# Three feed-forward layers as one hand-ordered list, eight column pairs by seven products for eight

## The chip, the cores and the metric

The kernel runs on one core of a Trainium2 chip. The number that counts is the device time of one execution in microseconds, as the median of several runs. Rows of the trace come from one profiled execution. In them PE is the matmul engine, PEld its loading of weights, DVE the vector engine, ACT the scalar engine, POOL the general engine; SP issues the transfers from memory.

## The reference

A diffusion backbone of two layers works on 256 noisy tokens with a prefix of 256 context tokens, width 1024. Each layer is a half-weighted SwiGLU feed-forward block (FFN), a mixer of three branches, and a second FFN; every sub-layer has a shift, a scale and a gate from a conditioning vector (nine modulations a layer). The last FFN needs the 256 noisy tokens only.

```python
def modulate(h, shift, scale):
    return h * (1.0 + scale) + shift

def swiglu(h, w1, w3, w2):
    return (jax.nn.silu(h @ w1) * (h @ w3)) @ w2
...
D_MODEL = 1024
SEQ = 256
DEPTH = 2
CTX_LEN = 256
D_FF = 2816
N_MOD = 9
```

## The kernel before

All is fp32. A factor x is split into x_hi, rounded, and x_lo = x - x_hi, and each product of 128 rows is three matmuls, hi·hi, lo·hi and hi·lo (`mm3`, L280 to L282). A block of weights of 512 KB (`wraw`) is loaded by SP, cast to `whi` by ACT (L285) and subtracted to `wlo` by DVE (L286). The tokens stand across: a matmul has 512 columns where an FFN works on all tokens, 256 where on half.

The hidden width 2816 is 11 column pairs of 256 columns of w1 and of w3. `ffn` takes six of them and then their part of the down product into the residual (`to_residual`), then the other five and theirs; the sum goes into `xT` with the gate `gmod` (L510), one group of 256 output columns at a time, four groups. The gated product `gt` (L616) is itself split into `ghi` and `glo`.

The modulations of later sub-layers are worked out in the background. `ada` loads 512 KB a step (`wada`), and a step is two DVE operations of 128x1024 (L208 the first, L210 the others); eight steps make a modulation, which the small product `pa` (L214), a copy `mrow` and four transposes (L219) then close. `tick` in `ffn` sets how many steps follow each unit of work; 16 modulations are done so, 6, 5 and 5 in the FFNs (0,0), (0,1) and (1,0).

The last output group of an FFN is the handover: products of half width, so that the norm of the first half of the tokens (`ms_f`, L319, then ACT and DVE to `hhi` and `hlo`) runs while PE does the second half, and then the first products of the next stage begin. In the handover the order on PE, DVE and ACT is that of the code; elsewhere a scheduler orders. The lines that set the work around `ms_f` are these:

```python
product(1, 0, 0, 5)
st.close(0)
product(1, 0, 5)
...
if i == 0:
    product(1, 1)
```

`product(t, d, a, b)` does the chunks a to b-1 of output half d for token half t, three matmuls a chunk; there are ten chunks in the last pass of `ffn`. `st.close(0)` issues `ms_f`.

Of the kernel before, what the change touches and what calls it, by code (L numbers as in the profile page):

```python
# [79 lines left out]
def dit_kernel(ctx: ExitStack, tc: tile.TileContext, I: dict, out: bass.AP):  # L80
# [4 lines left out]
    xp = ctx.enter_context(tc.tile_pool(name="xp", bufs=1))  # L85
    hp = ctx.enter_context(tc.tile_pool(name="hp", bufs=1))
    wr = ctx.enter_context(tc.tile_pool(name="wr", bufs=4))
    wh = ctx.enter_context(tc.tile_pool(name="wh", bufs=4))
    sm = ctx.enter_context(tc.tile_pool(name="sm", bufs=2))
    ps = ctx.enter_context(tc.tile_pool(name="ps", bufs=2, space=bass.MemoryType.PSUM))  # L90

    ctx.enter_context(tc.tile_pool(name="shift", bufs=1)).tile([P, 8], F32, name="shift")
# [15 lines left out]
    xr = [xi.tile([P, D], F32, name=f"xr{t}") for t in range(4)]  # L108
# [62 lines left out]
    def ada_first(q, c32):  # L171
# [3 lines left out]
        for k in range(0, KD, 2):  # L175
            ws.append(xi.tile([P, 2, 2, L], F32, tag="wada", name="wada", bufs=16))
            for m in range(2):
                sy.dma_start(ws[-1][:, :, m], rowsof(I["w_ada"][0], k, 2, m * D + q * L, L))
# [10 lines left out]
        mrow = xi.tile([P, P], F32, tag="mrow", name="mrow")  # L189
# [10 lines left out]
    def ada(l, m, pool):  # L200

        acc = pool.tile([P, 2, D], F32, tag="aacc", name="aacc")
        for k in range(KD):
            w = wr.tile([P, D], F32, tag="wr", name="wada")
            sy.dma_start(w, I["w_ada"][l, k * P:(k + 1) * P, m * D:(m + 1) * D])
            for t in range(2):
                if k == 0:
                    v.tensor_scalar_mul(acc[:, t], w, cs[:, k, t:t + 1])  # L208
                else:
                    v.scalar_tensor_tensor(acc[:, t], w, cs[:, k, t:t + 1], acc[:, t], op0=ALU.mult, op1=ALU.add)  # L210
            yield
        pa = psum_bg(f"pa{l}_{m}")
        for q in range(4):
            te.matmul(pa[32 * q:32 * q + 32, 0, :], ones32, acc[:, q % 2, (q // 2) * 512:(q // 2 + 1) * 512],  # L214
                      start=True, stop=True, tile_position=(0, 32 * q))
        mrow = pool.tile([P, 512], F32, tag="mrow", name="mrow")
        v.tensor_copy(mrow, pa[:, 0, :])
        for b in range(4):
            te.transpose(pa[:, 1, b * P:(b + 1) * P], mrow[:, b * P:(b + 1) * P], ident)  # L219
        v.tensor_tensor(modT[l][:, m].rearrange("p (h b) t -> p h b t", h=2),  # L220
# [4 lines left out]
        yield  # L225
# [34 lines left out]
    def split(srcs, nk, n, own=None, eng=v):  # L260

        pool, tag = own or (wh, "w")
        raw = load_raw(srcs, nk, n) if isinstance(srcs, list) else srcs
        if tag == "v":
            hi, lo = (pool.tile([P, 3, NTOK], F32R, tag=f"v{i}", name=x).rearrange("p a b -> p (a b)")[:, 0:nk * n]
                      .rearrange("p (k n) -> p k n", k=nk) for i, x in enumerate(("whi", "wlo")))
        else:
            hi = pool.tile([P, nk, n], F32R, tag=tag + "hi", name="whi")
            lo = pool.tile([P, nk, n], F32R, tag=tag + "lo", name="wlo")
# [55 lines left out]
    class Norm:  # L325

        def __init__(self, name, l, n, nt):
            self.name, self.l, self.n, self.nt = name, l, n, nt
            self.raw = {}

            self.shift = 48 if name in ("m1", "f11") else 0

        def places(self):
            self.hi, self.lo = (hp.tile([P, KD * NTOK + 256], F32R, tag=x, name=f"{x}_{self.name}")
# [191 lines left out]
    def load(w, kt, c0, r0=0, pool=None, tags=()):  # L526

        return [(split([rowsof(w, r0 + k, min(4, kt - k), c0, 2 * P)], min(4, kt - k), 2 * P,
                       pool and (pool, tags[k // 4])), k, min(4, kt - k))
                for k in range(0, kt, 4)]  # L530

    def to_residual(w, kt, x, nt, gate, st, pool, tags, r0=0, entry=None):

        for cg in range(4):
            if st is not None and cg == 3:
                chunks = load(w, kt, cg * 2 * P, r0, pool, tags)
# [38 lines left out]
    def ffn(l, f, nt, norm, mods, then):  # L575


# [3 lines left out]
        with tc.tile_pool(name=f"ffn{l}{f}", bufs=1) as fp:  # L581
            if nt == NTOK:
                fp.tile([P, 208], F32, name="pad0")
            for x in ("ghi", "glo"):
                fp.tile([P, 12, NTOK], F32R, tag=x, name=x)
            fp.tile([P, 208], F32, name="pad1")
            steps = (ada(*m, fp) for m in mods)
            pending[:] = [x for x in steps]
            total = len(mods) * (KD + 1)
            state = [0, 0]  # L590

            def tick():
                state[0] += 1
                want = min(total, -(-total * state[0] // 56))
                with norm.done():
                    background(want - state[1])
                state[1] = max(want, state[1])

            for half, (g0, g1) in enumerate(((0, 6), (6, 11))):
                nk = 2 * (g1 - g0)  # L600
                ghi = fp.tile([P, 12, NTOK], F32R, tag="ghi", name="ghi")
                glo = fp.tile([P, 12, NTOK], F32R, tag="glo", name="glo")
                for g in range(g0, g1):
                    p1, p3 = norm.accs if g == 0 else (psum("p1"), psum_bg("p3"))
                    if g > 0:
                        for acc, w in ((p1, w1), (p3, w3)):
                            product(acc, load(w, KD, g * 2 * P), (hhi, hlo), nt)
                            tick()
                            tick()
                    j = slice(2 * (g - g0), 2 * (g - g0) + 2)  # L610
                    gt = fp.tile([P, 2, NTOK], F32, tag="gt", name="gt")[:, :, 0:nt]
                    if g == 0 and norm.early:
                        norm.gated(gt)
                    else:
                        s.activation(gt, p1[:, :, 0:nt], AF.Silu)
                        v.tensor_tensor(gt, gt, p3[:, :, 0:nt], ALU.mult)  # L616
                    split_act(ghi[:, j, 0:nt], glo[:, j, 0:nt], gt)
                for _ in to_residual(w2, nk, (ghi, glo), nt, gmod[l][:, f], st if half else None, fp, ("a", "b", "c"), 2 * g0,
                                     then):
                    tick()  # L620
# [73 lines left out]
    def mixer(l, nq, entry, then):  # L694
# [35 lines left out]
        with tc.tile_pool(name=f"mx{l}", bufs=1) as mp:  # L730
            if shared:
                mp.tile([P, 208], F32, name="pad")
            br = [mp.tile([P, n, nq], F32, name=f"br{i}_{l}") for i, n in enumerate((2, 3, 3))]
# [39 lines left out]
            dk = [mq.tile([P, NTOK], F32, name=f"dk{j}") for j in range(3)]  # L773
# [53 lines left out]
            rv = mq.tile([P, 4, HEADS * DV], F32, tag="v0", name="rv")  # L827
# [9 lines left out]
            dv = mq.tile([P, 4, HEADS * DV], F32, name="dv")  # L837
# [3 lines left out]
            dq = [mq.tile([P, nq], F32, name=f"dq{j}") for j in range(3)]  # L841
# [190 lines left out]
            def merged(n, get, pool):  # L1032
                w, nk = wb[n]
                bh = pool.tile([P, 3, NTOK], F32R, tag="v0", name="bh")[:, 0:nk, 0:nq]
                bl = pool.tile([P, 3, NTOK], F32R, tag="v1", name="bl")[:, 0:nk, 0:nq]
# [170 lines left out]
```

## Time and profile before

| | us |
|---|---|
| median of 3 runs | 1994.27 (1992.68 to 1994.87) |
| profiled execution | 2003.08 |
| its span in the trace | 2001.3 |

The profiled execution is 0.44% longer than the median; the trace's span leaves out 1.8 us around it. PE is busy 1970.8 us of the span, DVE 1331.5, ACT 836.5. The mean granted clock of PE is 0.994 of full speed.

### The profile page before, as it was taken

The page shows a single profiled execution, that of the slowest core. Times are in us where ns is not written, and L with a number is a line of the kernel's source. Part 1 is how long each engine was busy: PE and PEld are TensorE (multiplying, and loading weights), DVE is VectorE, ACT ScalarE, POOL GpSimd, SP SyncE. Part 2 cuts the span into 40 slices and gives each one's busy share as a digit, 9 for nine tenths or more (in the row PEclk, how much of TensorE's full clock was granted, in tenths as well). Part 3 has the DMA queues.
Part 4 walks back from the last instruction along what each step waited for, and adds up shares of the span by engine and source line. Part 5 has one row for each costly group of instructions (what it writes and reads, how often), then busy time and mean ns, then how long its engine had stood idle before and what let it go on. Part 6 is the DMA issues. An engine that isn't in the chain of part 4 may idle for free.

```text
span 2001.3 us, 27970 instructions
## 1 busy us (share of the span) xinstructions
PE 1970.8 (98%) x11087; PEld 1684.3 (84%) x11087; DVE 1331.5 (67%) x2038; ACT 836.5 (42%) x1286; POOL 52.2 (3%) x32
## 2 busy tenths in 40 slices
PE   7999999999999999999999999999999998999998
PEld 5888888898777788988888898888888988899998
DVE  5876666576588655765666566664665779877555
ACT  3432222365476444422122343222223758666443
POOL 2000000000001110000000000000000001210000
PEclk8999999999999999999999999999999999999999
DMA  9755555422213324354555426554553234465663
GB/s 289 220 178 178 179 166 181 116 96 84 77 53 94 123 89 120 118 163 148 179 169 158 137 74 187 177 154 136 158 169 105 75 95 129 144 203 161 187 185 113
DMA packets 240507, 288.47 MB, mean 144 GB/s; under 512 B 14368, under 2 KB 222328, under 8 KB 240120
## 3 DMA queue, kind: packets, MB, share of 16 engines
q1 hardware_dynamic: 240376, 286.69, 46.7%
q8 instruction: 87, 1.43, 0.3%
q14 instruction: 44, 0.36, 0.1%
HBM read 283.50 MB, written 3.15 MB: 143 GB/s over the span
## 4 chain that ended last, share of the span: by engine, by line
PE 91%; DVE 4%; ACT 2%; DMA 2%; issue 1%; POOL 0%; SPq 0%; DVEq 0%; ACTq 0%; POOLq 0%
PE p L280 14%; PE p L282 14%; PE p L281 14%; PE py L280 8%; PE py L282 8%; PE py L281 8%; PE pg L282 3%; PE pg L281 3%; PE pg L280 3%; PE pj L281 2%; PE pj L280 2%; PE pj L282 2%; PE pv L819 1%; PE pv L821 1%; PE pv L820 1%
## 5 line engine op out<-in xcount | busy, mean ns | idle before, releaser
L285 ACT CAST whi<-wraw 128x1024 fp32r<-128x1024 f32 (+2 forms) x408 | 406.9, 1002 | 931.9 <-PE p L281 399.0
L286 DVE TENSOR_TENSOR wlo<-wraw,whi 128x1024 fp32r<-128x1024 f32 (+2 forms) x380 | 444.9, 1176 | 341.0 <-ACT whi L285 339.9
L280 PE MATMUL p<-hhi_f,whi 128*128 128x512 f32 (+1 forms) x1440 | 515.6, 358 | 0.4 <-DVE hhi_f L355 0.4
L282 PE MATMUL p<-hhi_f,wlo 128*128 128x512 f32 (+1 forms) x1440 | 512.9, 356 | 1.2 <-DVE wlo L286 0.7
L281 PE MATMUL p<-hlo_f,whi 128*128 128x512 f32 (+1 forms) x1440 | 513.5, 357 | 0.2
L280 PEld LDWEIGHTS p<-hhi_f,whi 128*128 128x128 f32 x1440 | 271.1, 188 | 48.3 <-ACT whi L285 5.9
L282 PEld LDWEIGHTS p<-hhi_f,wlo 128*128 128x128 f32 x1440 | 271.1, 188 | 41.0 <-POOL wlo L286 1.3
L281 PEld LDWEIGHTS p<-hlo_f,whi 128*128 128x128 f32 x1440 | 272.4, 189 | 39.0 <-DVE hlo_f L360 1.0
L210 DVE SCALAR_TENSOR_TENSOR aacc<-wada,cs,aacc 128x1024 f32<-128x1024 f32 x224 | 277.2, 1279 | 42.0 <-DMA wada<-w_ada 41.8
L280 PE MATMUL py<-ghi,whi 128*128 128x512 f32 (+1 forms) x764 | 266.9, 349 | 0.0
L281 PE MATMUL py<-glo,whi 128*128 128x512 f32 (+1 forms) x764 | 265.5, 347 | 0.0
L282 PE MATMUL py<-ghi,wlo 128*128 128x512 f32 (+1 forms) x764 | 265.3, 347 | 0.0
L280 PEld LDWEIGHTS py<-ghi,whi 128*128 128x128 f32 x764 | 143.4, 188 | 23.0 <-issue 4.2
L281 PEld LDWEIGHTS py<-glo,whi 128*128 128x128 f32 x764 | 144.5, 189 | 18.1
L282 PEld LDWEIGHTS py<-ghi,wlo 128*128 128x128 f32 x764 | 143.6, 188 | 18.3
L280 PE MATMUL pg<-hhi_m,whi 128*128 128x512 f32 (+1 forms) x384 | 132.4, 345 | 0.0
L282 PE MATMUL pg<-hhi_m,wlo 128*128 128x512 f32 (+1 forms) x384 | 130.3, 339 | 1.4 <-DVE wlo L286 1.4
L281 PE MATMUL pg<-hlo_m,whi 128*128 128x512 f32 (+1 forms) x384 | 130.1, 339 | 0.0
L286 POOL TENSOR_TENSOR wlo<-wraw,whi 128x768 fp32r<-128x768 f32 (+2 forms) x28 | 52.0, 1862 | 1722.2 <-ACT whi L285 1669.0
L510 DVE SCALAR_TENSOR_TENSOR xT<-py,gmod,xT 128x256 f32<-128x256 f32 x136 | 59.0, 477 | 51.8 <-PE py L282 51.4
L281 PE MATMUL pj<-hlo_m,whi 128*128 128x256 f32 (+1 forms) x288 | 92.3, 320 | 0.3 <-DVE hlo_m L360 0.2
L280 PE MATMUL pj<-hhi_m,whi 128*128 128x256 f32 (+1 forms) x288 | 92.4, 321 | 0.0
(270 smaller groups left out, 2528.6 us busy)
## 6 DMA issues: line engine op xcount, KB each, us to landing
wraw<-ffn_w SPq DMA_DIRECT2D x256, 512.0 KB, 3.9
wada<-w_ada SPq DMA_DIRECT2D x128, 512.0 KB, 3.7
wraw<-w_in SPq DMA_DIRECT2D x64, 512.0 KB, 3.6
wada<-w_ada SPq DMA_DIRECT2D x32, 256.0 KB, 6.9
wraw<-w_out SPq DMA_DIRECT2D x16, 512.0 KB, 3.5
wraw<-w_in SPq DMA_DIRECT2D x16, 384.0 KB, 3.4
wraw<-w_in SPq DMA_DIRECT2D x20, 256.0 KB, 3.0
wraw<-ffn_w SPq DMA_DIRECT2D x16, 256.0 KB, 2.7
```

Source lines behind the costliest of these rows:

```text
L210: v.scalar_tensor_tensor(acc[:, t], w, cs[:, k, t:t + 1], acc[:, t], op0=ALU.mult, op1=ALU.add)
L280: te.matmul(o, a, xh, start=start, stop=False)
L281: te.matmul(o, a, xl, start=False, stop=False)
L282: te.matmul(o, b, xh, start=False, stop=stop)
L285: s.copy(hi, src)
L286: eng.tensor_tensor(lo, src, hi.bitcast(F32), ALU.subtract)
L510: v.scalar_tensor_tensor(X[0][:, d, c], acc, gate[:, d, t:t + 1], X[0][:, d, c], op0=ALU.mult, op1=ALU.add)
L819: te.matmul(o, hhi[:, kk, ts], hi[:, k], start=(kk == 0), stop=False)
L820: te.matmul(o, hhi[:, kk, ts], lo[:, k], start=False, stop=False)
L821: te.matmul(o, hlo[:, kk, ts], hi[:, k], start=False, stop=(kk == KD - 1))
```

## The change

The three FFNs on 512 tokens become `ffn_both`; the fourth keeps the old plan. `ffn_both` builds one list of units of 24 matmuls, and `pipeline` issues it with the order on PE, DVE and ACT as written: the splits for a unit are issued three units ahead, at most three loads are outstanding, and DVE's background steps are dealt out by a `cost` of each unit.

- Column pair 0 is done in the handover as before, pairs 1 and 2 as ordinary units of 512 columns. Pairs 3 to 10 are done by `seven`: a product of 2 by 2 blocks by seven block products in place of eight, in the form with 15 additions. A block product is 24 matmuls of 256 columns.
- The sums of weight blocks are s1 and s3, made by a transfer that adds into its destination (issued by POOL after SP's plain load of the same tile), and s2 and s4, made by DVE. The forms of the tokens (`Forms`) are made once an FFN. Results of block products are copied by ACT (`keep`) and added by DVE (`add`).
- The down product is in three passes, after pairs 3, 7 and 10, of 8, 8 and 6 chunks; the last group of the third is the handover.
- A modulation is closed in pieces (`ada_end`), one per unit, in the list. In the first two FFNs the first residual needs a gate whose steps are forced in before it (`need`). The modulations are now 4, 2 (at the end of the first mixer), 5 and 5.
- Pools are laid out anew; `wr`, which holds raw loads, has 5 places for 4.

```diff
+    def seven(fm, wa, wb, c0, fp, done):
...
+        def both(tag, first, second):
+
+            t = x[tag] = fp.tile([P, 4, 2 * P], F32, tag=tag, name=tag, bufs=2)
+            sy.dma_start(t, rowsof(first[0], 4 * first[1], 4, c0, 2 * P))
+            gp.dma_start(t, rowsof(second[0], 4 * second[1], 4, c0, 2 * P), accum_op=ALU.add)
...
+        cost = 0.14
+        return [
+            Unit(part("b", fm.b11, True), whole("a11"), first_loads, 1, 0, [keep("q1", "b")], cost=cost),
+            Unit(part("c", fm.t1, True), whole("s1"), None, 0, 0, [keep("p5", "c")], cost=cost),
+            Unit(part("b", fm.t2), summed("s2", "s1", "a11"), None, 0, 1, [keep("w1", "b")], cost=cost),
+            Unit(part("a", fm.b21, True), whole("a12"), raw("a12", wa, 1), 1, 0, [add("q1", "a")], [silu(0, "q1")], cost=cost),
+            Unit(part("b", fm.t3), whole("s3"), None, 0, 0, [add("p5", "b")], cost=cost),
+            Unit(part("c", fm.b22), summed("s4", "s2", "a12"), None, 0, 1, [add("w1", "c")], [silu(1, "w1")], cost=cost),
+            Unit(part("b", fm.t4), whole("a22"), raw("a22", wb, 1), 1, 1, [gate(0, "b"), gate(1, "p5")],
+                 [lambda: done(x["gt"])], cost=cost)]
...
+            units = ordinary(1) + ordinary(2)
+            for c0, c1 in ((3, 4), (4, 8), (8, 11)):
+                g0 = 0 if c0 == 3 else c0
+                for c in range(c0, c1):
+                    units += seven(fm, w1, w3, c * 2 * P, fp, to(c - g0))
+                for cg in range(4 if c1 < KF // 2 else 3):
+                    units += down(cg, 2 * g0, 2 * (c1 - g0), c1 == KF // 2, KD if first and cg == g0 == 0 else None)
```

The loop of `pipeline`, which sets the order at each unit (`now` of the unit before, the next splits, the closing pieces, the background steps, `end` of the unit before, the unit's matmuls):

```diff
+            for i in range(len(units) + 1):
+                prev = units[i - 1] if i else None
+                if prev:
+                    if prev.need is not None:
+                        while did < prev.need and step():
+                            did += 1
+                        finish(True)
+                    for f in prev.now:
+                        f()
+                while pi < min(len(units), i + 4):
...
+                    units[pi].w = units[pi].prep()
...
+                finish()
+                if i < len(units):
+                    want += units[i].cost * scale
+                    while did < min(total, int(want + 1e-6)) and step():
+                        did += 1
+                if prev:
+                    for f in prev.end:
+                        f()
```

On DVE one column pair of the FFN (0,1) looked like this before (one gate `gt`, four splits `wlo`, the split `glo`, and adaLN products `aacc`):

```order
L286 TENSOR_TENSOR wlo<-wraw,whi 128x1024
L210 SCALAR_TENSOR_TENSOR aacc<-wada,cs,aacc 128x1024 x3
L286 TENSOR_TENSOR wlo<-wraw,whi 128x1024
L210 SCALAR_TENSOR_TENSOR aacc<-wada,cs,aacc 128x1024
L616 TENSOR_TENSOR gt<-gt,p_7318 128x1024
L286 TENSOR_TENSOR wlo<-wraw,whi 128x1024
L286 TENSOR_TENSOR glo<-gt,ghi 128x1024
```

With the change, in the same FFN, one column pair of `seven` reads so (`s_...` are tiles with added loads, `half_...` and `w_...` hold sums and kept results, L739 is a sum of weights, L761 an add, L776 a gate):

```order
L325 TENSOR_TENSOR wlo<-wraw,whi 128x1024
L240 SCALAR_TENSOR_TENSOR aacc<-wada,cs,aacc 128x1024 x2
L761 TENSOR_TENSOR half_7676<-p_8798,half_7676 128x512
L325 TENSOR_TENSOR wlo<-s_8782,whi 128x1024
L761 TENSOR_TENSOR w_7677<-p_8798,w_7677 128x512
L739 TENSOR_TENSOR half_7676<-s_8782,wraw 128x1024
L325 TENSOR_TENSOR wlo<-half_7676,whi 128x1024
L776 SCALAR_TENSOR_TENSOR gt<-p_8798,gt 128x2x256
L776 SCALAR_TENSOR_TENSOR gt<-half_7676,gt 128x2x256
L325 TENSOR_TENSOR wlo<-wraw,whi 128x1024
L325 TENSOR_TENSOR glo<-gt,ghi 128x1024
L325 TENSOR_TENSOR wlo<-s_8787,whi 128x1024
```

A sum L739 and the split of its result stand next to each other, and adds and gates from PSUM stand between the splits.

Still on DVE in the FFN (0,1), this is the place of the first pass of the down product up to its first residual, L547; it begins with the gates of column pair 3:

```order
L776 SCALAR_TENSOR_TENSOR gt<-half_7676,gt 128x2x256
L325 TENSOR_TENSOR wlo<-wraw,whi 128x1024
L240 SCALAR_TENSOR_TENSOR aacc<-wada,cs,aacc 128x1024 x2
L325 TENSOR_TENSOR glo<-gt,ghi 128x1024
L325 TENSOR_TENSOR wlo<-wraw,whi 128x1024
L240 SCALAR_TENSOR_TENSOR aacc<-wada,cs,aacc 128x1024 x6
L257 COPY mrow<-pa_8_8294 128x512
L262 TENSOR_TENSOR modT_117<-pa_8_8294,biasT_118 128x16
L190 TENSOR_SCALAR gmod_123<-modT_117 128x16
L547 SCALAR_TENSOR_TENSOR xT<-py,gmod_123,xT 128x256 x4
```

The last three steps of the modulation stand together ahead of the residual that uses its gate. Before, this modulation was closed among the column pairs, long before the first residual.

On PE the end of the same pass reads so (`py` is the down product, `p_...` the first unit of the next column pair):

```order
L319 MATMUL py<-ghi,whi 128x512
L320 MATMUL py<-glo,whi 128x512
L321 MATMUL py<-ghi,wlo 128x512
L253 MATMUL pa_0_8554<-aacc,ones_107 32x512 x4
L753 MATMUL p_8559<-hhi_f_7218,whi 128x256
L753 MATMUL p_8559<-hlo_f_7219,whi 128x256
L753 MATMUL p_8559<-hhi_f_7218,wlo 128x256
```

Before, the same product stood among matmuls of one down group:

```order
L280 MATMUL py<-ghi,whi 128x512
L281 MATMUL py<-glo,whi 128x512
L282 MATMUL py<-ghi,wlo 128x512
L214 MATMUL pa_0_7660<-aacc,ones_102 32x512 x4
L280 MATMUL py<-ghi,whi 128x512
L281 MATMUL py<-glo,whi 128x512
```

It has moved to the end of the pass. What DVE does ahead of it, from the residual of the third output group to that of the fourth, is this with the change:

```order
L547 SCALAR_TENSOR_TENSOR xT<-py,gmod_123,xT 128x256 x4
L325 TENSOR_TENSOR wlo<-s_8342,whi 128x1024
L240 SCALAR_TENSOR_TENSOR aacc<-wada,cs,aacc 128x1024 x2
L739 TENSOR_TENSOR half_7676<-s_8342,wraw 128x1024
L325 TENSOR_TENSOR wlo<-half_7676,whi 128x1024
L240 SCALAR_TENSOR_TENSOR aacc<-wada,cs,aacc 128x1024 x4
L547 SCALAR_TENSOR_TENSOR xT<-py,gmod_123,xT 128x256 x4
```

The splits here already belong to the next column pair, and the last two steps of the modulation stand behind them.

## Rows read from the trace of the kernel before

**Rows 1.** The page: busy time by engine, and the chain that ended last.

```profile
PE 1970.8 (98%) x11087; PEld 1684.3 (84%) x11087; DVE 1331.5 (67%) x2038; ACT 836.5 (42%) x1286; POOL 52.2 (3%) x32
...
PE 91%; DVE 4%; ACT 2%; DMA 2%; issue 1%; POOL 0%; SPq 0%; DVEq 0%; ACTq 0%; POOLq 0%
```

**Rows 2.** Windows by stage: FFN (0,0), mixer, FFN (0,1), FFN (1,0).

```profile
core 0: us, PE busy (x) PEld busy (x) DVE busy (x) ACT busy (x) POOL busy (x), PEclk, DMA share, GB/s
48.00:400.00 352.00, 351.48 (x1612) 286.98 (x1613) 245.72 (x319) 105.46 (x118) 0.47 (x1) 1.00 0.58 175
412.00:806.00 394.00, 390.56 (x1962) 319.43 (x1961) 263.70 (x503) 213.84 (x392) 20.84 (x12) 1.00 0.29 92
806.00:1184.00 378.00, 377.48 (x1860) 315.07 (x1860) 238.56 (x291) 115.95 (x149) 0.00 (x0) 1.00 0.48 148
1188.00:1555.00 367.00, 367.00 (x1781) 305.14 (x1781) 229.61 (x266) 109.12 (x133) 0.00 (x0) 1.00 0.50 151
```

**Rows 3.** Timeline of the handover after the FFN (0,1): start, length.

```profile
1172.55 0.64 PE L319 MATMUL ms_f<-acc_f,ones 128*128 128x256 f32 x2
...
1172.84 0.47 PE L280 MATMUL py<-ghi,whi 128*128 128x256 f32 x1
...
1173.22 0.47 ACT L290 ACTIVATE acc_f<-ms_f,eps 128x256 f32<-128x256 f32 x1 [1.25 <-PE ms_f L319]
...
1173.73 0.42 DVE L291 SCALAR_TENSOR_TENSOR rtmp<-ms_f,acc_f 128x256 f32<-128x256 f32 x1 [1.30 <-ACT acc_f L290]
...
1175.11 1.43 DVE L341 TENSOR_TENSOR h<-xT,acc_f 128x256 f32<-128x256 f32 x4
...
1177.51 0.75 DVE L360 TENSOR_TENSOR hlo_f<-h,hhi_f 128x256 fp32r<-128x256 f32 x2
...
1178.33 0.28 PE L280 MATMUL p<-hhi_f,whi 128*128 128x256 f32 x1
```

**Rows 4.** Timeline of PE, two gapless stretches: their first and last products.

```profile
299.75 0.39 PE L280 MATMUL p<-hhi_f,whi 128*128 128x512 f32 x1
...
314.48 0.39 PE L282 MATMUL p<-hhi_f,wlo 128*128 128x512 f32 x1
...
1899.69 0.28 PE L281 MATMUL py<-glo,whi 128*128 128x256 f32 x1
...
1903.93 0.28 PE L281 MATMUL py<-glo,whi 128*128 128x256 f32 x1
```

**Rows 5.** Timeline of DVE in the FFN (1,0).

```profile
1331.62 1.65 DVE L510 SCALAR_TENSOR_TENSOR xT<-py,gmod,xT 128x256 f32<-128x256 f32 x4
1333.19 2.35 DVE L286 TENSOR_TENSOR wlo<-wraw,whi 128x1024 fp32r<-128x1024 f32 x2
...
1392.68 0.68 DVE L217 COPY mrow<-pa 128x512 f32<-128x512 f32 x1
...
1394.69 6.06 DVE L210 SCALAR_TENSOR_TENSOR aacc<-wada,cs,aacc 128x1024 f32<-128x1024 f32 x5
```

**Rows 6.** Groups by line and shape: busy us, mean ns of one, idle before.

```profile
L286 DVE TENSOR_TENSOR wlo<-wraw,whi 128x1024 fp32r<-128x1024 f32 x340 | 413.7, 1221 | 293.5 <-ACT whi L285 292.5
...
L1065 DVE SCALAR_TENSOR_TENSOR gt<-gt,pb 128x512 f32<-128x512 f32 x16 | 10.3, 684 | 13.6 <-PE pb L282 13.6
...
L285 ACT CAST whi<-wraw 128x1024 fp32r<-128x1024 f32 x344 | 360.4, 1052 | 843.4 <-PE p L281 387.5 <-PE py L281 218.7 <-DMA wraw<-ffn_w 120.7
```

**Rows 7.** Timeline of PE around the close of a modulation.

```profile
1390.26 0.39 PE L282 MATMUL p<-hhi_f,wlo 128*128 128x512 f32 x1
1390.58 1.06 PE L214 MATMUL pa<-aacc,ones 128*32 128x512 f32 x8
1391.58 0.50 PE L280 MATMUL p<-hhi_f,whi 128*128 128x512 f32 x1
```

**Rows 8.** Windows at the end of the first mixer, columns as in rows 2.

```profile
640.00:660.00 20.00, 20.00 (x97) 15.87 (x97) 17.43 (x28) 13.55 (x25) 3.75 (x2) 1.00 0.24 73
...
680.00:700.00 20.00, 18.94 (x89) 14.77 (x90) 9.99 (x23) 8.48 (x20) 1.83 (x1) 1.00 0.59 203
700.00:720.00 20.00, 20.00 (x85) 15.67 (x84) 14.81 (x20) 11.08 (x13) 1.86 (x1) 1.00 0.23 72
```

**Rows 9.** DMA: packets, queues, and issues by tile, KB each, us to landing.

```profile
DMA packets 240507, 288.47 MB, mean 144 GB/s; under 512 B 14368, under 2 KB 222328, under 8 KB 240120
...
q1 hardware_dynamic: 240376, 286.69, 46.7%
...
wraw<-ffn_w SPq DMA_DIRECT2D x256, 512.0 KB, 3.9
...
wada<-w_ada SPq DMA_DIRECT2D x32, 256.0 KB, 6.9
```

More of the change, by code (lines that the diff above doesn't have):

```diff
@@ L224, in ada @@
         modulated(l, m)
-        yield
     pending = []
@@ L573, in ffn_entry, with __init__, pipeline, step @@
                      [(psum, "p1", 2), (psum_bg, "p3", 2)], early=(nt == L))
-    def ffn(l, f, nt, norm, mods, then):
+    class Unit:
+        def __init__(self, mm, prep, load=None, takes=0, gives=0, now=(), end=(), cost=1.0, need=None):
+            self.mm, self.prep, self.load, self.takes, self.gives = mm, prep, load, takes, gives
+            self.now, self.end, self.cost, self.need = now, end, cost, need
+    def pipeline(units, fills, steps, total, made):
+        eng = mybir.EngineType
+        scale = total / sum(u.cost for u in units[:-3])
+        li = pi = out = did = 0
+        want = 0.0
+        def step():
+            return next(steps, "end") != "end"
+        def finish(everything=False):
+            while made:
+                if next(made[0], "end") == "end":
+                    made.pop(0)
+                if not everything:
+                    return
+        with tc.manual_schedule(engines={eng.PE, eng.DVE, eng.Activation}):
+            for i in range(len(units) + 1):
[8 more added lines that the diff above has]
+                while pi < min(len(units), i + 4):
+                    while li < len(units) and (li <= pi or out + units[li].takes <= 3):
+                        if units[li].load:
+                            units[li].load()
+                        out += units[li].takes
+                        li += 1
+                    units[pi].w = units[pi].prep()
+                    out -= units[pi].gives
+                    pi += 1
+                for f in fills.get(i, ()):
+                    f()
[6 more added lines that the diff above has]
+                    for f in prev.end:
+                        f()
+                if i < len(units):
+                    units[i].mm(units[i].w)
+            while step():
+                pass
+            finish(True)
@@ L578, in ffn @@
+    def ffn(l, f, norm, then):
         hhi, hlo = norm.hi, norm.lo
@@ L606, in ffn @@
                         for acc, w in ((p1, w1), (p3, w3)):
[L607 to L612, printed above, removed]
-                        norm.gated(gt)
[L614 to L620, printed above, removed]
+                            product(acc, load(w, KD, g * 2 * P), (hhi, hlo), L)
+                        s.activation(gt, p1[:, :, 0:L], AF.Silu)
+                        v.tensor_tensor(gt, gt, p3[:, :, 0:L], ALU.mult)
+                    else:
+                        norm.gated(gt)
+                    split_act(ghi[:, j], glo[:, j], gt)
+                run(to_residual(w2, 2 * (g1 - g0), (ghi, glo), L, gmod[l][:, f], st if g0 else None, fp, weights, 2 * g0, then))
         return st
@@ L1168, in dit_kernel @@
     entry = mixer_entry(0)
-    ffn(0, 0, NTOK, after, [(0, m) for m in range(2, 8)], entry)
+    ffn_both(0, 0, after, [(0, m) for m in range(2, 6)], entry, True)
     load_mixer_consts()
```

334 lines of the change are left out of this document (263 added, 71 removed).

## The prediction

> **What bounds the kernel now.** I read the page's engine totals first [rows 1]: the matmul engine is busy 98% of the span, the vector engine 67%, and the chain that ended last runs 91% through PE. The windows by stage say where [rows 2]: in the FFN of layer 1 (the fourth window) PE is busy 367.00 of 367 us, and DVE 229.61, 63%. So PE sets the time, and an edit pays in two ways only: fewer PE microseconds, or fewer holes in PE; it costs where DVE, which now has room, must deliver something that PE's next instruction needs. The handover to the next stage is the place where PE's cover is already thin [rows 3]: the first new product starts 0.07 us after the last split it reads.
>
> **The gain.** A product of 512 columns starts 0.2266 us after the one before it (65 steps from 299.75 to 314.48), one of 256 columns 0.1178 us after (36 steps from 1899.69 to 1903.93) [rows 4]; the "0.39" and "0.28" are each product's own length and overlap. An ordinary column pair has 4 units of 24 products of 512 columns, 96 x 0.2266 = 21.76 us; the new one 7 units of 24 of 256 columns, 168 x 0.1178 = 19.79 us. Seven eighths would be 19.04; the missing 0.75 is what a short product costs extra. The gain is 1.97 us a column pair, and 24 of them (8 in each of three FFNs) give **-47.2 us**. The units' additions, casts and copies lie on DVE and ACT beside it, if these keep up.
>
> **Does DVE keep up?** Back to back a split of 128x1024 takes DVE 1.14 us (second of two in 2.35), an adaLN product 1.2 (five in 6.06, so 2.4 for a step, which has two), the four residual adds 1.65, a copy of 128x512 0.68 [rows 5]; a gate from PSUM is 0.68 long, 0.65 back to back, and ACT's cast 1.05 [rows 6]. One new column pair is seven splits, two sums of weights and the split of the gated tile, ten at 1.14 = 11.4; three adds and two gates from PSUM, five at 0.65 = 3.2; and two waits of 1.1 for the cast, since a sum on DVE is cast on ACT and then subtracted by DVE, with nothing between in DVE's list (the second order block). That is 16.8, and with 1.1 adaLN steps 19.5 against PE's 19.8: it just holds. ACT has about 11.4 and is not in question. A column group of down product is 48 products of 512, 10.88 us on PE; DVE has 1.65 + 2 x 1.14 + 2.96 steps x 2.4 = 11.0 where five modulations are spread over an FFN. It just does not hold. Over the FFN of the fourth window DVE goes from 229.6 to about 330 us (eight times the 9.8 that a new column pair has over an ordinary one's four splits, gate and glo; 6.6 for four more residual groups; 15 for the token forms) of 367 - 16 = 351, so the total fits, but the list is fixed, and where it is dense PE waits. I walked DVE's rows with these durations through the dense places:
>
> *Handovers.* After the norm's ms product, PE has the rest of the last column group as cover: 15 + 30 = 45 products of 256, 5.3 us, from 1172.84 to 1178.33 [rows 3]. The last pass has six chunks where it had ten, so 3 + 18 = 21 remain, 2.5 us, while the chain ms, reciprocal root, h, hi, lo is as long as before. PE stands 3.0 us; three FFNs: **+9.0**.
>
> *The first residual's gate.* In the first two FFNs the first residual of the down product needs a modulation that isn't finished, and the list forces its last steps there. In the third order block: the two gates, split, one step, then glo is 6.0 us after the column's end, against 5.44 for the unit that runs; then a split and six adaLN products, 8.4, end at 14.4, when PE has been through since 11.5; pa's consumers add 0.9 (the copy 0.68 and its way back). That is 0.6 + 2.9 + 0.9 = 4.4, and with eight adaLN products in the first FFN, 2.4 later, 6.8: **+11.2**.
>
> *The ends of the other modulations.* pa, the product that closes a modulation, stands in PE's list directly behind the last unit of a pass (the fourth order block), and DVE finishes its input late: from the residual of the third column group on, 1.65 + 1.14 + 2.4 + 1.14 + 1.1 + 1.14 + 4.8 = 13.4 against 10.9 of PE. 2.5 late there, by the same count 2.8 at the end of the second pass and 2.6 in the third: 7.9 an FFN, in the two FFNs with five: **+15.8**. Before, pa shows no idle time in front of it [rows 7].
>
> *The last column's split.* Between the last gate of a pass and glo, DVE has a split and two adaLN steps in the second pass: 1.3 + 1.14 + 4.8 + 1.14 = 8.4 against 5.44, 2.9 late, twice; 0.6 in the first pass of the third FFN: **+6.4**.
>
> *Smaller.* Two modulations, 32 adaLN products, move into the end of the first mixer, where DVE has 17.43 of 20 us and then 10 to 15 [rows 8]: hidden but for about **+2**; a chain of tiny 128x12 operations stands inside a column of the first FFN: **+2**.
>
> Sum: -47.2 + 9.0 + 11.2 + 15.8 + 6.4 + 4.0 = -0.8. Against the profiled execution's 2003.08 us that is 2002.3; the median of the runs shown is 0.44% lower, so **1993.5 us**, no change that can be told: 0.2%, 4 us, is about what a measurement of this kernel tells from none.
>
> **Bounds of what the trace does not show.** No transfer that adds into its destination is in it. Each new column pair has two, each 512 KB behind a plain load of the same tile. The nearest row, a plain 512 KB weight load, lands after 3.9 us; the slowest, the first modulation's loads, after 6.9 [rows 9]. The lead from issue to the split that needs the tile is about 14 us of list, with 8 more of splits already made, so 3.9 + 3.9 or 3.9 + 6.9 are hidden; I take nothing. POOL is idle but for 52 us [rows 1], so its queue adds no wait that these rows show. Traffic grows by 3 x 512 KB a column pair, 38 MB on 288 [rows 9]; at 46.7% of the engines that is hidden.
>
> **Rivals.**
> (a) DVE's lead absorbs the pass ends. A unit's split is listed three units ahead, 8.5 us in a column and 16 in a down pass; if DVE enters each pass with that lead whole, residuals and adaLN run early too, and only the handovers and the forced gate, 20.2 us, remain: 2003.08 - 47.2 + 20.2 = 1976.1, median 1967. Against it: the residual waits for PE, so the 13.4 us are counted from there, with no backlog.
> (b) DVE is the bound through the columns, the other side. Its adds wait for PE's unit in DVE's list, and the splits queue behind. If it then takes ten splits at their full length of 1.22 instead of the pitch of 1.14 [rows 6], a column pair is 20.3, 0.5 over PE's 19.8, and 24 x 0.5 = 12 come on top: about 2005. It decides from 19.8 us of DVE a column pair.
> (c) The adding transfers come late. From about 10 us each on, every microsecond is paid 24 times; at 12 us, 2 x 24 = 48 more: 2041. The Trainium skill's page SBUF — State Buffer, section "SBUF: two separate sides", warns of just this: a transfer issued from GpSimd has its descriptors written by GpSimd's cores, which are locked out while DVE runs a two-port fast-mode operation. By that rule the transfers would wait in DVE's dense stretches. No row here has such a transfer; the splits' 1.14 us for 1024 elements a partition is 1.1 ns each, which does not look like a fast mode.
> (d) The short products don't hold 0.1178 with three new token forms: at 0.13, 168 x 0.0122 x 24 = 49 more. The pitch is the same in rows whose weights change each product [rows 4], so I give it little.
>
> **How the numbers follow.** The forecast's own range is 1985 to 2002 (stalls between 38 and 55 us): chance 0.37, of which 0.14 lies over 0.2% below, 0.15 within, 0.08 above. (a), with everything between 1955 and 1985: 0.30. (b), 2002 to 2018: 0.20. (c) 0.10, (d) 0.03. So faster 0.44, same 0.15, slower 0.41. The range leaves out (c), (d) and the lower end of (a): 1963 to 2018.
>
> **What the profile after would show.** Right: 24 stretches of 168 short products, 19.8 us each; idle time of PE before the first product of a handover of about 3 us, released by hlo; idle before pa of 2.5 to 3 us, released by aacc; DVE near 90% in the three FFN windows. Wrong: PE's waits there under 1 us (a); PE waiting for wlo or for a sum's add inside the columns (b); ACT or DVE waiting on DMA for s (c); a short product over 0.12 us (d).

## The result, and the profile after

The changed kernel takes 2138.65 us, median of 4 runs (2131.97 to 2139.34), against 1993.63 for the kernel before in the same session (1992.68 to 1994.87): 1.072 times as long, interval 1.0697 to 1.0742. No change was forecast, 1963 to 2018 the range. The profiled execution has a span of 2137.4 us.

The page, busy time by engine, for [rows 1]; and the windows by stage for [rows 2], each FFN with its own new length:

```profile
PE 1978.2 (93%) x12743; PEld 1733.8 (81%) x12743; DVE 1580.8 (74%) x2338; ACT 962.6 (45%) x1466; POOL 116.4 (5%) x80
```

```profile
48.00:452.00 404.00, 358.96 (x2212) 312.89 (x2211) 297.17 (x397) 148.89 (x183) 20.91 (x16) 0.97 0.60 161
452.00:858.00 406.00, 400.49 (x2020) 324.08 (x2019) 307.34 (x554) 215.90 (x397) 21.76 (x12) 1.00 0.36 113
858.00:1274.00 416.00, 372.75 (x2358) 324.26 (x2357) 315.32 (x372) 154.34 (x199) 20.77 (x16) 0.97 0.61 166
1280.00:1692.00 412.00, 373.09 (x2352) 325.41 (x2351) 314.87 (x372) 154.26 (x199) 19.45 (x15) 0.98 0.59 159
```

PE, which had no hole in an FFN, is idle for 39 to 45 us in each, and its granted clock is 0.97 there. DVE is at 74 to 76%, well short of full: no engine is saturated. So PE waits for something in order, not for throughput. Groups of instructions by line (busy us, mean ns, idle before, releaser) name it:

```profile
L753 PE MATMUL p<-hhi_f,whi 128*128 128x256 f32 x768 | 222.3, 289 | 47.4 <-DVE half L761 26.4 <-DVE w L761 21.0
...
L753 PE MATMUL p<-zone,whi 128*128 128x256 f32 x1152 | 212.8, 287 | 43.1 <-ACT half L758 43.1
...
L253 PE MATMUL pa<-aacc,ones 128*32 128x512 f32 x128 | 34.9, 752 | 25.1 <-DVE aacc L240 24.5
```

90.5 of the idle us are in the columns of seven products, ahead of the first matmul of a unit, and what ends them is ACT's copy (L758) or DVE's add (L761) that reads an accumulator. Timeline of PE over one such column pair in the FFN (0,1), only the rows with idle time ahead; then ACT's copy:

```profile
1173.47 0.38 PE L753 MATMUL p<-hhi_f,whi 128*128 128x256 f32 x1 [0.78 <-DVE half L761]
1177.33 0.36 PE L753 MATMUL p<-hhi_f,whi 128*128 128x256 f32 x1 [0.88 <-DVE w L761]
...
1183.77 0.50 PE L753 MATMUL p<-zone,whi 128*128 128x256 f32 x2 [0.73 <-ACT half L758]
...
1187.43 0.51 PE L753 MATMUL p<-zone,whi 128*128 128x256 f32 x2 [0.68 <-ACT half L758]
...
1196.66 0.38 PE L753 MATMUL p<-hhi_f,whi 128*128 128x256 f32 x1 [0.78 <-DVE half L761]
1200.63 0.36 PE L753 MATMUL p<-hhi_f,whi 128*128 128x256 f32 x1 [0.88 <-DVE w L761]
```

```profile
1183.13 0.59 ACT L758 COPY half<-p 128x512 f32<-128x512 f32 x1
```

These are four waits a column pair, 3.1 us, and 23.2 us from one pair to the next (1173.47 to 1196.66), here with no engine late: the copy starts when the unit ends, lasts 0.59, and PE starts 0.05 after it (1183.72 to 1183.77). But the unit that waits writes accumulator c, and the copy reads b. In the code both are halves of one tile: `x["b"], x["c"], x["a"] = pab[:, 0], pab[:, 1], pc[:, 0]`. In the mean of the 24 pairs, from the first product of a pair to the end of its last, a pair takes 25.0 us.

Elsewhere the add is late too, and PE's granted clock falls after the wait. Windows of 2 us (PE, PEld, DVE, ACT, POOL, then the granted clock, DMA share and GB/s), and three products in them:

```profile
1458.00:1460.00 2.00, 0.36 (x4) 0.16 (x2) 2.00 (x2) 1.05 (x1) 0.00 (x0) 1.00 0.79 207
1460.00:1462.00 2.00, 1.03 (x6) 1.03 (x7) 2.00 (x3) 0.00 (x0) 0.00 (x0) 0.82 1.11 159
1462.00:1464.00 2.00, 2.00 (x11) 2.00 (x11) 0.05 (x1) 0.00 (x0) 0.00 (x0) 0.50 0.94 248
1464.00:1466.00 2.00, 1.58 (x11) 1.38 (x10) 0.38 (x1) 0.00 (x0) 0.00 (x0) 0.83 0.17 59
```

```profile
1460.97 0.39 PE L753 MATMUL p<-hhi_f,whi 128*128 128x256 f32 x1 [2.61 <-DVE half L761]
...
1463.03 0.41 PE L753 MATMUL p<-hlo_f,whi 128*128 128x256 f32 x1
1463.25 0.41 PE L753 MATMUL p<-hhi_f,wlo 128*128 128x256 f32 x1
```

After 2.61 us of idleness the granted clock is at its lower level, 1.2 GHz, for 3.4 us, and the products there are 0.21 apart.

Where the stages stand, from the starts of the norms' ms products (us; FFN (0,0) from the span's start to its ms, the others from the second ms of one handover to the first of the next; each row is one profiled execution, and that of e5, 2052.8 us, lies 14 us over e5's median):

| kernel | FFN (0,0) | mixer 0 | FFN (0,1) | FFN (1,0) | mean clock |
|---|---|---|---|---|---|
| before | 400.4 | 390.4 | 359.1 | 359.0 | 0.994 |
| changed | 443.3 | 397.2 | 404.7 | 400.1 | 0.979 |
| e4, list only | 417.4 | 396.4 | 376.6 | 371.0 | 0.993 |
| e5, regrouped | 414.1 | 396.3 | 377.7 | 370.6 | 0.984 |
| e6, little adaLN | 398.7 | 396.3 | 346.5 | 344.3 | 0.995 |
| e9 | 393.4 | 397.0 | 363.6 | 363.4 | 0.992 |
| e11 | 394.3 | 407.6 | 349.4 | 363.3 | 0.990 |
| e12 | 391.7 | 407.3 | 346.7 | 348.7 | 0.991 |

### The profile page after: what moved, and what is told of

Its sections match the earlier page's. It is cut to its first block, busy times and chain, and to the rows that moved or that the text cites. A ratio compares the mean times of both kernels' runs of the same rounds, so it can differ in the third digit from the quotient of the medians.

```text
span 2137.4 us, 32048 instructions
## 1 busy us (share of the span) xinstructions
PE 1978.2 (93%) x12743; PEld 1733.8 (81%) x12743; DVE 1580.8 (74%) x2338; ACT 962.6 (45%) x1466; POOL 116.4 (5%) x80
## 5 line engine op out<-in xcount | busy, mean ns | idle before, releaser
L753 PE MATMUL p<-hhi_f,whi 128*128 128x256 f32 x768 | 222.3, 289 | 47.4 <-DVE half L761 26.4
L753 PE MATMUL p<-zone,whi 128*128 128x256 f32 x1152 | 212.8, 287 | 43.1 <-ACT half L758 43.1
L319 PE MATMUL p<-hhi_f,whi 128*128 128x256 f32 (+1 forms) x672 | 216.2, 322 | 2.3 <-DVE hhi_f L392 2.3
L753 PE MATMUL p<-hlo_f,whi 128*128 128x256 f32 x768 | 217.3, 283 | 0.0
L753 PE MATMUL p<-hhi_f,wlo 128*128 128x256 f32 x768 | 217.0, 283 | 0.0
L321 PE MATMUL p<-hhi_f,wlo 128*128 128x256 f32 (+1 forms) x672 | 215.0, 320 | 1.1 <-DVE wlo L325 0.6
L320 PE MATMUL p<-hlo_f,whi 128*128 128x256 f32 (+1 forms) x672 | 215.5, 321 | 0.5 <-DVE hlo_f L397 0.2
L319 PE MATMUL py<-ghi,whi 128*128 128x512 f32 x492 | 194.4, 395 | 0.0
L320 PE MATMUL py<-glo,whi 128*128 128x512 f32 x492 | 192.8, 392 | 0.6 <-DVE glo L325 0.5
L321 PE MATMUL py<-ghi,wlo 128*128 128x512 f32 x492 | 192.1, 391 | 0.0
```

What stands on the lines that cost most here:

```text
L319: te.matmul(o, a, xh, start=start, stop=False)
L320: te.matmul(o, a, xl, start=False, stop=False)
L321: te.matmul(o, b, xh, start=False, stop=stop)
L753: te.matmul(om, wt[w][:, k, cm], form[f][:, k], start=(first and k == m == n == 0), stop=(k == 3 and m == 1 and n == 2), skip_group_check= ...
```

## The experiments

Theory 1: the accumulators' shared tile makes each unit wait until the last one has been read. Rivals: the adding transfers come late (theory 2), DVE is too dense (theory 3).

**e1: a tile each, from two rings; pa from the other ring.**

```diff
-                    pab, pc = psum("p1"), psum_bg("p3")
-                    x["b"], x["c"], x["a"] = pab[:, 0], pab[:, 1], pc[:, 0]
+                    x["b"], x["c"], x["a"] = psum("p1")[:, 0], psum_bg("p3")[:, 0], psum_bg("p3")[:, 0]
...
```

> The three accumulators b, c and a of a column pair get a PSUM tile each (before, b and c were the two halves of one tile), and the closing product pa takes the other ring of tiles. The computation is the same. Theory 1 (shared tile: a unit that writes one half waits until the other half has been read by ACT or DVE): PE's waits for the copies L758 (43 us) and for the adds L761 (26 and 21 us) nearly vanish, and so does most of the half-speed clock behind the longest of them; 90 to 130 us less, 2010 to 2050. Theory 2 (the adding transfers come late): no change, 2130 to 2145. Theory 3 (DVE is too dense, the adds and copies are late because their engines are): the waits move to the next unit that needs the same accumulator, at most 40 us less, 2100 to 2140.

2072.79 us (1.036 times before, 1.0324 to 1.0394), 66 under the changed kernel: below what either rival allowed, but above the 2010 to 2050 of theory 1. The waits in the columns nearly vanish (groups by line):

```profile
L752 PE MATMUL p<-hhi_f,whi 128*128 128x256 f32 x768 | 217.0, 283 | 7.3 <-DVE xT L547 3.9 <-DVE half L760 3.4
...
L752 PE MATMUL p<-zone,whi 128*128 128x256 f32 x1152 | 203.2, 279 | 7.3 <-ACT half L757 5.3 <-ACT w L757 1.6
...
L319 PE MATMUL py<-ghi,whi 128*128 128x512 f32 x492 | 197.5, 401 | 19.6 <-DVE xT L547 19.0 <-DVE modT L262 0.5
```

The third row is new: pa now takes a tile of the ring that the down products use, and these wait for the residual, 19 us. The waits did what theory 1 says; that the miss in the time is the price of pa's new place is argued here. e5 does without that change.

**e2: no adding transfer.** The second term of s1 and s3 is left out.

```diff
-            gp.dma_start(t, rowsof(second[0], 4 * second[1], 4, c0, 2 * P), accum_op=ALU.add)
```

> The second, adding transfer of s1 and s3 is left out, so that these sums hold only their first term; all else as in the changed kernel. Theory 1 (shared tile): within 15 us of 2138. Theory 2 (adding transfers late): nearly all of the loss comes back, below 2040. Theory 3 (DVE): within 15 us of 2138.

2130.1 us (1.066, 1.0623 to 1.0695), 8.6 less: theory 2, by which nearly all of the loss should come back, is out. In the changed kernel an adding transfer lands after 6.8 us, its plain load after 5.2, the other weights after 4.2 (issues by tile):

```profile
wraw<-ffn_w SPq DMA_DIRECT2D x232, 512.0 KB, 4.2
...
s<-ffn_w SPq DMA_DIRECT2D x48, 512.0 KB, 5.2
s<-ffn_w POOLq DMA_DIRECT2D x48, 512.0 KB, 6.8
```

**e3: little adaLN.** Six of eight steps of the modulations in the FFNs are not added up.

```diff
-                else:
+                elif made is None or k == KD - 1:
```

> In the FFNs only the first and the last of the eight steps of a modulation are added up, so 168 of DVE's adaLN products (some 200 us of DVE) are left out; the loads stay. Theory 1 (shared tile): PE's waits for ACT's copies (43 us) stay whole, those for DVE's adds, for pa's input (32 us with pa) and for the forced gate shrink: 2060 to 2095. Theory 2: within 20 us of 2138. Theory 3 (DVE): below 2030.

2067.15 us (1.034, 1.0307 to 1.038), 71 less. As theory 1 says, the waits in the columns stay, 39.0 and 34.1 us of the 47.4 and 43.1, and those before pa go, 0.5 of 25.1:

```profile
L753 PE MATMUL p<-hhi_f,whi 128*128 128x256 f32 x768 | 219.1, 285 | 39.0 <-DVE w L761 21.0 <-DVE half L761 18.0
...
L753 PE MATMUL p<-zone,whi 128*128 128x256 f32 x1152 | 209.1, 284 | 34.1 <-ACT half L758 34.1
...
L253 PE MATMUL pa<-aacc,ones 128*32 128x512 f32 x128 | 19.4, 605 | 0.5 <-DVE aacc L240 0.4
```

So DVE's density is a second cause beside the tile, not another name for it.

**e4: the list without the seven products** (and without the token forms).

```diff
...
-                    units += seven(fm, w1, w3, c * 2 * P, fp, to(c - g0))
+                    units += ordinary(c, c - g0)
...
```

> The new list with its splits three ahead, its three down passes and its modulations closed in pieces, but column pairs 3 to 10 as ordinary units of 512 columns (28 units of 24 short products in place of 32 of long ones undone); no adding transfers, no token forms. The computation is the same. By the terms of the prediction the list costs 9.0 for the handovers, 11.2 for the forced gate and some of the 22 for modulations' ends and the last split: 2010 to 2035. If it costs nothing, 1990 to 2000, and everything lost is lost in the columns of seven products.

2044.34 us (1.023, 1.0194 to 1.0265), 48 over before: more than expected. The list alone costs about what the prediction gave it for all its waits (46.4), though with fewer of them: pa's waits are 9.5 us here. In the FFN (0,1), 17.5 us over, PE is idle for 5.5 us (2.85 of it before pa, 0.8 before the transposes), with the granted clock at 1.00 throughout; pa itself takes 2.16 us instead of 1.06, and 2.8 of handover work now lie ahead of ms:

```profile
935.32 2.16 PE L253 MATMUL pa<-aacc,ones 128*32 128x512 f32 x8 [2.85 <-DVE aacc L240]
```

Another 6.5 us are the pitch of the long products (the time from the start of one to the start of the next): 63% of them start over 0.230 us after the one before, against 3% in the kernel before, at the same granted clock. What sets that pitch no run shows; it comes back under *The gain* below.

**e5: the same tiles, regrouped.** b alone; c and a, which are never neighbours, in the other.

```diff
-                    x["b"], x["c"], x["a"] = pab[:, 0], pab[:, 1], pc[:, 0]
+                    x["b"], x["c"], x["a"] = pab[:, 0], pc[:, 0], pc[:, 1]
```

> The same number of tiles as in the changed kernel, regrouped: b has a tile to itself, c and a are the halves of the other, so that no unit writes the tile that the unit just before it wrote; pa keeps its ring. Shared-tile theory: a column pair without backlog on DVE took 23.2 us and should take 19.8; 24 x 3.4 = 82 less, and with the longer waits for adds (2.6 us, and the half-speed clock behind them) 85 to 105: 2035 to 2055. If e1's gain came from elsewhere (from pa's ring), 2060 or more.

2038.62 us (1.0203, 1.0173 to 1.0232): one line is worth 100 us. The columns' waits are 5.0 and 8.1 us, and the mean column pair takes 20.9 us for 25.0:

```profile
L753 PE MATMUL p<-hhi_f,whi 128*128 128x256 f32 x768 | 217.4, 283 | 5.0 <-DVE half L761 5.0
...
L753 PE MATMUL p<-zone,whi 128*128 128x256 f32 x1152 | 204.3, 280 | 8.1 <-ACT half L758 6.3 <-ACT w L758 1.6
```

In some column pairs DVE now has no room left. The timeline of one from gate to gate, 1018.57 to 1038.94, is 20.4 us with one adaLN step; DVE idles for 3.0 us of it, 2.6 before casts have ended, while PE waits 1.56 for an add:

```profile
1018.57 0.68 DVE L776 SCALAR_TENSOR_TENSOR gt<-p,gt 128x512 f32<-128x512 f32 x1
...
1025.95 1.23 DVE L325 TENSOR_TENSOR wlo<-half,whi 128x1024 fp32r<-128x1024 f32 x1 [1.17 <-ACT whi L324]
...
1028.52 2.48 DVE L240 SCALAR_TENSOR_TENSOR aacc<-wada,cs,aacc 128x1024 f32<-128x1024 f32 x2
...
1037.80 1.22 DVE L325 TENSOR_TENSOR wlo<-half,whi 128x1024 fp32r<-128x1024 f32 x1 [1.19 <-ACT whi L324]
1038.94 0.68 DVE L776 SCALAR_TENSOR_TENSOR gt<-p,gt 128x512 f32<-128x512 f32 x1
```

**e6: e5 with e3's edit.**

> e5 with six of the eight steps of each modulation in the FFNs left out (not added up; loaded all the same), some 200 us of DVE's work. If DVE's density in the lists is what remains of the loss (late pa, late glo, late residuals, and the slow clock behind each), it is 50 to 75 us under e5, 1965 to 1995, and the kernel with it is faster than before. If the rest is in the handovers and in the transfers, within 25 us of e5.

1977.12 us (0.9898, 0.9862 to 0.9935), 62 under e5 and faster than before. The FFNs (0,1) and (1,0) are 12.6 and 14.7 us shorter than before; the clock is 0.995. What e5 lost is DVE's density and what follows from it, and most of that is outside the columns: the mean column pair falls from 20.9 us to 20.0 only, 24 x 0.9 = 22 us. At the ends of passes, e5 had 29.3 us of idle time before pa and 6.0 before glo's products:

```profile
L320 PE MATMUL py<-glo,whi 128*128 128x512 f32 x492 | 194.4, 395 | 6.0 <-DVE glo L325 6.0
L253 PE MATMUL pa<-aacc,ones 128*32 128x512 f32 x128 | 34.5, 766 | 29.3 <-DVE aacc L240 28.8
```

In e6 they are 5.4 and nothing, and PE's clock is at its lower level for 21.0 us of the span where it was 66.2 in e5.

**e7: e5 with glo first and more steps in the ordinary units.** In the loop of `pipeline` the block `if prev: for f in prev.end: f()` goes ahead of the background steps, and:

```diff
-                        more = {"cost": 0.6 if c > 1 else 0}
+                        more = {"cost": 1.4 if c > 1 else 0}
```

> e5 with two changes of DVE's list: the split glo of a column's last gates stands ahead of the background steps, and the ordinary units get more background steps (cost 1.4 for 0.6), so that fewer are forced before the first residual and fewer stand in the down passes. By the sum of the prediction 6.4 for glo and some 7 of the forced gate's 11.2, and the slow clock behind them: 12 to 25 us under e5. If only DVE's whole load matters and not its order, within 6 us of e5.

2021.29 us (1.0119, 1.008 to 1.0159), 17 under e5, as expected; which of the two changes brought how much was not separated.

**e8: e5 with pa one unit later.**

```diff
+        if unclosed:
+            yield
         pa = psum_bg(f"pa{l}_{m}")
...
-                    while did < min(total, int(want + 1e-6)) and step():
+                    while not unclosed and did < min(total, int(want + 1e-6)) and step():
```

> e5 with pa issued one unit later, and no background step until it is issued, so that PE has a unit to do while DVE ends pa's input. If the waits before pa are a matter of place, they vanish, 15.8 by the sum and some 2 us of slow clock behind each of six: 15 to 28 us under e5. If DVE is late whatever stands there, the wait moves to the next residual or split: within 8 us of e5.

2025.65 us (1.0141, 1.0102 to 1.0181), 13 under e5, a little less than the 15 to 28 expected: pa's waits in the FFN (0,1) fall from 4.06, 2.88, 2.07 and 2.04 to 4.09 (the forced one), 0.19 and 0.52, but some come back at the next step, 1.25 and 2.59 before the transposes.

**e9: e7 and e8 together.**

> The regrouped accumulators with both changes of the lists, glo ahead of the background steps with more steps in the ordinary units, and pa one unit later. If the waits they took away are different ones, their gains against e5 (17 and 13 us) add up: 2005 to 2015. If DVE's whole load sets the time, the second brings little: 2017 to 2022. Still slower than before in both.

2009.48 us (1.0048, 1.0032 to 1.0065), 29 under e5: the gains add up.

**e10: e9 with the sums on POOL.**

```diff
-                v.tensor_tensor(x[name], x[a], x[b], ALU.add)
+                gp.tensor_tensor(x[name], x[a], x[b], ALU.add)
```

> e9 with the sums s2 and s4 made by POOL instead of DVE, 48 operations of 1.2 us off DVE and as many of about 2.6 us on POOL; the 1.2 us in which DVE waits for the cast of a sum can be spent too. If DVE's density is what is left, 48 x 2.4 us = 115 us of DVE's time come free and the time falls by 10 to 30 us against e9, to the time of before or under it. If POOL's sums come late (they queue with the adding transfers), splits wait for them: 10 us or more slower than e9.

2026.16 us (1.0129, 1.0112 to 1.0146), 17 slower than e9: a miss for theory 3 as I applied it. DVE is not relieved: it is busy 1586.4 us here and 1575.0 in e9. Groups by line and shape of DVE, in e9 and then in e10:

```profile
L331 DVE TENSOR_TENSOR wlo<-wraw,whi 128x1024 fp32r<-128x1024 f32 x307 | 374.4, 1221 | 143.1 <-ACT whi L330 137.9 <-PE pf L1202 3.5 <-PE p L759 0.6
L240 DVE SCALAR_TENSOR_TENSOR aacc<-wada,cs,aacc 128x1024 f32<-128x1024 f32 x224 | 280.8, 1298 | 2.7 <-DMA wada<-w_ada 2.7
```

```profile
L331 DVE TENSOR_TENSOR wlo<-wraw,whi 128x1024 fp32r<-128x1024 f32 x307 | 396.6, 1293 | 163.3 <-ACT whi L330 159.0 <-PE pf L1202 3.5
L240 DVE SCALAR_TENSOR_TENSOR aacc<-wada,cs,aacc 128x1024 f32<-128x1024 f32 x224 | 301.9, 1391 | 1.9 <-DMA wada<-w_ada 1.8
...
L767 DVE TENSOR_TENSOR half<-p,half 128x512 f32<-128x512 f32 x48 | 32.8, 683 | 6.2 <-PE p L759 6.0
```

The same operations became longer, these two kinds by 43 us, while an add with an input from PSUM kept its 0.68. The timeline of e10 shows how, DVE and then POOL:

```profile
1340.28 4.45 DVE L331 TENSOR_TENSOR wlo<-wraw,whi 128x1024 fp32r<-128x1024 f32 x1
```

```profile
1340.72 2.91 POOL L745 TENSOR_TENSOR half<-s,wraw 128x1024 f32<-128x1024 f32 x1
```

A split of 1.22 us took 4.45 while a sum ran on POOL. The Trainium skill's page SBUF — State Buffer, section "SBUF: two separate sides", says that DVE and GpSimd share a pair of ports as a lock, also for DVE operations with two inputs from SBUF against a GpSimd one that reads it; these rows agree. The rival on record, that POOL's sums come late, is not borne out on the whole: ACT's casts of them wait 15.6 us for POOL, where in e9 they waited 150.6 for DVE. But these are four waits of 3.8 to 4.2 us, and what they cost behind them was not separated. So that the lock is all of the 17 us is argued, not shown.

**e11: the second FFN's gate in the first mixer too** (modulations 4, 3, 4, 5; the mixer gets more background steps a unit).

```diff
-    ffn_both(0, 1, after, [(0, 8)] + [(1, m) for m in range(4)], entry, True)
+    ffn_both(0, 1, after, [(1, m) for m in range(4)], entry, False)
...
```

> e9 with the modulation of the second FFN's gate done in the first mixer too (three there, four in that FFN), so that nothing is forced before that FFN's first residual. DVE density theory: that FFN gains 4 to 8 us, the mixer, where two modulations cost some 7 us, loses 3 to 6: within 5 us of e9, its stages shifted by so much.

2004.6 us (1.0027, 1.001 to 1.0044), 5 under e9, with intervals that overlap: the FFN gains 14 us, the mixer loses 10, both more than expected.

**e12: the last gate in the fourth FFN** (4, 3, 4, 4 and 1 there, one step after each product).

```diff
-    ffn_both(1, 0, entry, [(1, m) for m in range(4, 9)], after, False)
+    ffn_both(1, 0, entry, [(1, m) for m in range(4, 8)], after, False)
...
```

> e11 with the last modulation, the gate of the fourth FFN, done in that FFN itself instead of the third (4, 3, 4, 4 and 1). DVE density theory: the third FFN, 4 us slower than before with five modulations, becomes 6 to 10 us faster than before with four, as the first two are; the fourth FFN, where DVE is busy 60%, loses 1 to 5: 6 to 13 us under e11, that is level with the kernel before or up to 0.5% under it. If the number of modulations is not what sets a stage's time, within 3 us of e11.

1993.04 us over 12 runs, against 1998.66 for before over 17 in the same session: 0.9983 (0.9967 to 0.9999), under the changed kernel by far and under the one before by a hair. The FFN (1,0) falls by 14.6 us to 348.7. From its ms to the end of the span it is 456.8 us here and 457.5 in e11, but that does not make the moved modulation free: PE is idle 2.9 us in the fourth FFN, for 0.6 in e11, and its granted clock is 0.99 for 1.00. What hides this is the pitch of the short products, 0.1158 us in the mean here and 0.1178 in e11; at one pitch the modulation costs some 4 us, an estimate from these figures.

## Why the prediction was wrong

*The step that failed* is "it just holds", with "That is 16.8, and with 1.1 adaLN steps 19.5 against PE's 19.8". It compared what DVE has to do in a column pair with what PE has to do, and never asked in which order each waits for the other. The units' accumulators share a tile, so four of seven units start only after the one before has been read: 23.2 us a column pair where DVE is not late, 25.0 in the mean, not 19.8. The regrouping alone took 100 us off. In the traces the mean pair falls from 25.0 to 20.9 us, 24 x 4.1 = 98: 77 of it are the waits themselves (90.5 before, 13.1 after), the rest lies in the clock behind them and the pitch. None of the rivals was this: (b) came nearest, but priced DVE's throughput. It could be read beforehand: the change gives six of the seven units to accumulators b and c, and the second order block names one tile, `p_8798`, for the adds that read them.

*"Does DVE keep up?"* was too tight on its own terms too: with one adaLN step a column pair takes DVE 20.4 us, where 16.8 + 2.4 = 19.2 were counted; three small waits beside the two that were seen, one for a cast and two for PE, 0.7 us together, make over half of the difference. That is rival (b), but its share is small: with little adaLN (e6) the mean pair is only 0.9 us shorter, some 22 of the 62 us. The sign "DVE near 90%" did not come either, 74 to 76% did: the stages were longer, and the sum of 330 us had taken DVE's own waits, 2.2 a pair, for work (314.9 measured in the FFN (1,0)).

*The gain.* Short products in a column can be closer than [rows 4] said: 21 steps from 1184.10 to 1186.48, 0.113 us each.

```profile
1184.10 0.28 PE L753 MATMUL p<-zone,wlo 128*128 128x256 f32 x1
...
1186.48 0.28 PE L753 MATMUL p<-zone,wlo 128*128 128x256 f32 x1
```

At that pitch 168 take 19.0 us, seven eighths of 21.76 exactly, and the gain would have been 24 x 2.7 = 65, not 47.2. So a short product costs nothing extra; [rows 4] set a long product in one stretch beside a short one in a stretch of another pitch. Both pitches occur in one kernel at the same granted clock; the trace of before has short products 0.113 us apart from 1650 to 1800 us and 0.118 after that. In e6 these are two windows of three column pairs each, without a hole (columns as in [rows 2]):

```profile
172.30:231.60 59.30, 59.30 (x505) 59.30 (x504) 43.67 (x45) 30.44 (x37) 7.78 (x6) 1.00 0.74 178
966.80:1023.80 57.00, 57.00 (x506) 57.00 (x505) 45.21 (x46) 33.83 (x41) 6.72 (x6) 1.00 0.88 228
```

That is 0.1178 and 0.1133 us a product, 19.8 and 19.0 a pair. The fourth FFN, whose code is the same in e9 and e10, took 185.6 us in e9 at the one and 179.3 in e10 at the other, so a few us between two experiments can be this alone. What sets the pitch stays open. Rival (d), over 0.12, is out.

*Handovers*, 3.0 us each, for [rows 3]:

```profile
1267.82 0.70 PE L358 MATMUL ms_f<-acc_f,ones 128*128 128x256 f32 x2 [0.69 <-DVE acc_f L351]
...
1272.87 0.35 PE L319 MATMUL p<-hhi_f,whi 128*128 128x256 f32 x1 [1.88 <-DVE hhi_f L392]
```

0.69 + 1.88 = 2.6: nearly right in size. The larger part is in the place that was named, but it is hhi that ends it, not hlo; the 0.69 ahead of ms was not foreseen.

*The forced gate and the ends of modulations*, for [rows 7], in the FFN (0,1):

```profile
962.54 3.03 PE L253 MATMUL pa<-aacc,ones 128*32 128x512 f32 x8 [3.04 <-DVE aacc L240]
...
1002.91 1.05 PE L253 MATMUL pa<-aacc,ones 128*32 128x512 f32 x2 [3.21 <-DVE aacc L240]
...
1154.68 1.04 PE L253 MATMUL pa<-aacc,ones 128*32 128x512 f32 x2 [2.08 <-DVE aacc L240]
...
1246.24 3.12 PE L253 MATMUL pa<-aacc,ones 128*32 128x512 f32 x8 [2.08 <-DVE aacc L240]
```

2.9, 2.5, 2.8 and 2.6 were counted; 3.04, 3.21, 2.08 and 2.08 came. What was left out is that pa itself gets longer: it takes 3.03 and 3.12 us at the lower clock, and 2.16 in e4 at full clock, instead of 1.06. *The last column's split*, 6.4, was 0.6 us in the changed kernel, but 6.0 in e5 without the shared tile, where pa's waits were 29.3 against 2.9 + 5.3 + 15.8 = 24.0 counted for them. So these terms were roughly right for a list without the shared tile. *The chain of 128x12 operations*, 2, is about 3: the column pair with it takes 23.0 us in e6, its neighbours 19.8.

*The clock* had no term at all. Over the span it is 0.979 for 0.994. The traces hold only the two levels, and the lower one for 91.0 us, against 27.2 before, so 64 more at half speed: an estimate of some 30 us lost.

*The adding transfers* (rival c): 3.9 to 6.9 was the bracket, 6.8 came, nearly hidden as taken. The Trainium skill's warning (SBUF — State Buffer, section "SBUF: two separate sides") does not decide here: without these transfers the kernel is only 8.6 us faster.

*The mixer*, with the two modulations in it, lost 6.8 us, not 2.

## What to carry to other kernels

When work is cut into shorter units, look at who must have read the accumulator before the next unit may write, and give neighbours in time different tiles; in these kernels the dependence was between tiles, whatever half was used. A sum of busy times per unit shows whether a plan can hold, not whether it does: walk the waits in order, and beside each longer wait of PE count the lower clock that can follow it. Before two pitches are set against each other, look whether the trace has more than one pitch for the same products. And background work belongs where an engine has room: moving two of sixteen modulations took the ratio from 1.0048 to 0.9983. POOL was no such place: with sums on it, DVE's own operations became longer.

## What the runs showed of the hardware

A wait of 2 to 3 us in PE's stream can cost more than itself: in one column pair of the changed kernel 2.61 us idle was followed by 3.4 us at a granted clock of 0.50, with products 0.21 us apart, and the pair took 26.6 us, 1.8 more of it idle and 1.5 more busy than in one of 23.3. It does not always: after 2.85 us in e4 the clock stayed at 1.00. At that same full clock short products ran 0.1133 or 0.1178 us apart in long stretches of one kernel (e6), cause open. A transfer that adds into its destination landed 6.8 us after its issue, 1.6 more than the plain load of the same size just before it. And a sum of 128x1024 on POOL, 2.9 us, stretched a DVE operation with two inputs from SBUF from 1.22 to 4.45 us.
